# A chunked gated recurrence: two tree levels' matmuls per visit of the tensor engine, and two weight blocks split earlier and on another engine

## The chip, the cores and the metric

The kernel runs on one core of a Trainium2 chip. The time is device microseconds of one execution of the whole program. The kernel before takes 1827.11 us, the median of 3 runs (1826.62 to 1827.6).

## The reference, cut to what matters

The program is one step of a two-layer trunk on 640 tokens (128 context, 512 latent) of width 1024. Layer 0 mixes tokens by attention, layer 1 by a gated linear recurrence (HGRN2); each is followed by a dense feed-forward part. The change is inside layer 1's mixer. Cut to its core, the reference computes there, for each of 8 heads and for both directions:

```python
def chunk_gla(q, k, v, lf, s0):            # c = 16 tokens a chunk
    b = jnp.cumsum(lf, axis=2)             # lf = log(f), f the forget gate, k = 1 - f
    dec = exp(b[t] - b[s])  for s <= t
    a = sum(q[t] * k[s] * dec, over dk)    # all pairs inside a chunk
    o = a @ v + (q * exp(b)) @ s_start     # pairs inside, and the state before
    s = exp(b_last) * s + (k * exp(b_last - b)).T @ v
def hgrn_project(h, w_in, lb):
    q, vi, g, zf, zb = split(h @ w_in, 5)  # query, value, output gate, two forget gates
    f = lb + (1 - lb) * sigmoid(z)
def hgrn_mix(...):                         # forward scan plus the scan of the reversed tokens
```

Any chunk length gives the same result, and the kernel uses chunks of 128 tokens.

## The kernel before, in words

All of `hgrn` (line 1029) handles one head at a time: 128 channels on the partitions, 640 tokens in five tiles of 128 on the free axis. `project` (1040) makes a head's inputs, and `core` (1123) computes its recurrence. Both are generators. While `core(h)` of one head runs, `project(h + 1)` of the next is the filler: each `yield n` of `core` makes the loop at 1285 take `n` units of the filler. TensorE runs in exactly the order in which the program issues it (`pe["strict"]`), so these numbers are TensorE's order. The other engines' orders are chosen by a scheduler at build time; each engine then runs its queue strictly in that order.

**Weights.** Matmuls with weights keep close to float32 accuracy by splitting each raw block `wr` into a high part `wh` (`AC.activation`, ScalarE, ACT in the profile) and a low part `wl = wr - wh` (`split_raw`, 197), and using three products. The low part goes to GpSimd (POOL) in three pieces, or to VectorE (DVE) in one. A head has five blocks of 128x1024: two `ch` (query and forward gate), one `chb` (backward gate), two `cg` (value and output gate). There are 6 buffers each for `wh` and `wl`.

**The filler.** `project` makes six products `psf` of 24 matmuls (two halves of the tokens; query, forward gate, backward gate), each in 4 units, then five `psvg` (values and gates) of 24 matmuls, also 4 units each: 44 units. After a `psf`, ACT takes the sigmoid `sg`, and DVE makes `q`, or else the gate `F2`, the key `CD = 1 - F2` and the query times the gate, `Q2`. After a `psvg`, ACT copies `v` and takes the gate's sigmoid, and DVE multiplies (`gt`). `load_cg` (1053) for a head other than the first stands after the last `psf`. `psf` and `psvg` share 3 PSUM buffers.

**The recurrence.** `core` builds the 128x128 score matrix `A` of each token tile as a binary tree. First come the diagonal's products ("base": `q` with `kd`), then for levels li = 0 to 6 the pairs of neighbouring blocks of 2^li tokens: keys `C` times queries from `Q2`, 20 small matmuls of 32 columns (10 of 64 at level 6) into the PSUM tile `pa` (two buffers). Base and each level are one *visit* of TensorE, with 4 units of filler behind it: eight visits. After a level's products DVE folds its decays in: `Cn` (two instructions, two buffers), `CD`, and `Q2` in place, for which the level's products must have been read; and puts the level into `A` with `copy_predicated`. Levels 5 and 6 go into `A` by ACT, with copies of one part by POOL. POOL multiplies the decays of pairs (`T2`).

After level 6 come the transposes `ktp` in three groups (one PSUM buffer, read by ACT into `KT2`), then `pk` (the states) and five `po` (the output). POOL computes `rs`, and DVE writes the head's output `orow`.

**The last head** has no next projection: its filler is `part_units` (562), 22 units that turn `orow` (transposes `otp`, ACT's `Thi`, DVE's `Tlo`) and multiply with the output weights (`psr`, matmuls of 512 columns). The loop at 1303 takes 2 units a visit, 1 in some.

Names in the profile lose their numbers: `Q` is `Q2`, `F` is `F2`, `T` is `T2`, `KT` is `KT2`. Nearly all instructions of ACT, DVE and POOL carry line 51, and all matmuls line 96 (transposes 99), so a row is told by its tiles.

Of the kernel before, what the change touches and what calls it, by code (L numbers as in the profile page):

```python
# [21 lines left out]
P = 128  # L22
D = 1024
KT = D // P
NT = 5
# [34 lines left out]
def trunk_kernel(ctx: ExitStack, tc: tile.TileContext, I, O):  # L60
# [136 lines left out]
    def split_raw(r, lo_eng, ordered=False):  # L197
        n = r.shape[1]
        hi = wp.tile([P, 1024], F32R, name="wh", tag="wh", bufs=6)
        lo = wp.tile([P, 1024], F32R, name="wl", tag="wl", bufs=6)  # L200
        AC.activation(hi[:, :n], r, AF.Copy)
        parts = 3 if lo_eng is PO else 1
        for i in range(parts):
            cs = slice(n * i // parts, n * (i + 1) // parts)
            ins = lo_eng.tensor_tensor(lo[:, cs], r[:, cs], hi[:, cs], ALU.subtract)
            if ordered:
                tc.keep_in_program_order(ins)
        return hi[:, :n], lo[:, :n]
# [820 lines left out]
    def hgrn(regB, hT, o_tiles, xr):  # L1029
        with ExitStack() as sc:  # L1030
# [9 lines left out]
            def project(h):  # L1040
# [32 lines left out]
                if h == 0:  # L1073
                    load_cg()
# [43 lines left out]
                if h:  # L1118
                    load_cg()
# [3 lines left out]
            def core(h):  # L1123
# [4 lines left out]
                def pair_products(w, keys, queries):  # L1128
                    pa = psB.tile([P, 1024], F32, name="pa", tag="pa", bufs=2)
# [12 lines left out]
                def across(w):  # L1142
                    def queries(t, b):
                        c0 = t * P + w * (b ^ 1)
                        return Q2[:, 1 - b % 2, c0 : c0 + w]

                    return queries

                pa = pair_products(32, kd, lambda t, b: q[:, t * P + 32 * b : t * P + 32 * b + 32])
                AC.activation(Ad, pa, AF.Copy)  # L1150
                S = {}
                for d in range(2):
                    s0 = rp.tile([P, P], F32, name="s0", tag="S", bufs=8)
                    nc.sync.dma_start(out=s0, in_=st[d, h])
                    S[d, 1 if d == 0 else NT - 1] = s0
                yield 4
                T, n = F2, TOK
                C, Dk = CD[:, 0], CD[:, 1]
                for li in range(7):
# [3 lines left out]
                    qdims = ([2 * m, nb], [TOK + m, 2], [1, m])  # L1163
                    qview = view(Q2, 0, *qdims)
                    if li < 5:
                        bt = 32 // (2 * m)
                        pa = pair_products(32, C, lambda t, b: qview[:, (4 * t + b) * bt : (4 * t + b + 1) * bt])
                    else:
                        pa = pair_products(m, C, across(m))
                    if li < 6:  # L1170
                        Cn = rp.tile([P, TOK], F32, name="Cn", tag="Cn", bufs=2)
# [13 lines left out]
                        VE.tensor_tensor(  # L1185
                            qview, qview, view(T, n + 1, [2, nb], [-n - 1, 2], [0, m]), ALU.mult
                        )
                    else:
                        Cn = rp.tile([P, TOK], F32, name="Cn", tag="Cn", bufs=2)
# [6 lines left out]
                        VE.tensor_tensor(  # L1196
                            qview, qview, view(T, n + 1, [2, nb], [-n - 1, 2], [0, m]), ALU.mult
                        )
                    if li < 5:
                        VE.copy_predicated(Ad, masks[:, li, :].unsqueeze(1).to_broadcast([P, NT, 32]), pa)  # L1200
                    else:
                        for b in range(P // m):
                            rs_, own, other = slice(m * b, m * b + m), slice(0, m), slice(m, 2 * m)
                            if b % 2:
                                PO.tensor_copy(A[rs_, :, other], A[rs_, :, own])
                                AC.activation(A[rs_, :, own], pa[rs_], AF.Copy)
                            else:
                                AC.activation(A[rs_, :, other], pa[rs_], AF.Copy)
# [3 lines left out]
                    T, n, C = T2, nb, Cn  # L1212
                    yield 4
# [787 lines left out]
```

## Time and profile before

| | |
|---|---|
| median of 3 runs | 1827.11 us |
| profiled execution | 1824.8 us |
| its span | 1823.0 us |
| granted TensorE clock | 0.998 |
| busy share of the span: PE / DVE / ACT / POOL | 97% / 67% / 41% / 35% |
| recurrence, from the first head's base visit to the last one's | 958.1 to 1295.6 us |
| one head there | 48.2 us |

The last two rows are from the timeline of TensorE; the first head's base visit is its row that starts at 958.11. In a timeline row stand the start, the time from the first start to the last end of the instructions in it, the engine, the line, the operation, output and inputs, shape, the count, and in brackets how long the engine was idle before and what released it. A small float32 matmul counts twice (x40 for 20). A matmul's row lasts to its modelled end, while the next one starts before: how fast TensorE goes is read from starts. A windows row gives, for a stretch, its length, and each engine's busy time with the number of its instructions.

### The profile page before, as it was taken

To read this page: it belongs to the slowest core of one execution; us is meant where nothing else is said; L and a number is where in the kernel's file an instruction comes from. 1 tells how busy PE (TensorE), PEld (TensorE's weight loads), DVE (VectorE), ACT (ScalarE), POOL (GpSimd) and SP (SyncE) were. 2 spreads that over 40 slices of the span, in tenths; PEclk is the share of its full clock that TensorE was granted. 3 is DMA by queue.
4 is the path that set the end of the run, shared out by engine and by line. 5 is a ranking of instruction groups with operands and counts; after the bars stand their busy time and mean duration, and the time that the engine had idled before them with its cause. 6 is when DMAs were issued, how large, how long until landed. Compare 5 with 4: busy or idle time off the path is not lost.

```text
span 1823.0 us, 34717 instructions
## 1 busy us (share of the span) xinstructions
PE 1770.5 (97%) x13791; PEld 1626.0 (89%) x13791; DVE 1219.6 (67%) x2128; ACT 742.0 (41%) x1642; POOL 643.0 (35%) x750
## 2 busy tenths in 40 slices
PE   6999999999999999999999999999999999999997
PEld 5799999878898899899899999999879898998896
DVE  4888888756266755855667766666759656566666
ACT  3567666635132122122353333333345443433443
POOL 3344544325000000000056554444411557366562
PEclk9999999999999999999999999999999999999999
DMA  9511221454264534453442222211222324233331
GB/s 317 180 44 45 70 62 39 168 185 122 90 202 138 150 106 133 143 152 122 145 128 67 62 63 65 59 60 58 84 84 82 104 82 116 81 99 110 93 104 70
DMA packets 222857, 195.28 MB, mean 107 GB/s; under 512 B 10276, under 2 KB 176606, under 8 KB 222694
## 3 DMA queue, kind: packets, MB, share of 16 engines
q1 hardware_dynamic: 221888, 192.46, 34.2%
q8 instruction: 108, 1.77, 0.4%
q10 hardware_dynamic: 806, 0.60, 0.1%
q14 instruction: 55, 0.45, 0.1%
HBM read 185.64 MB, written 7.37 MB: 106 GB/s over the span
## 4 chain that ended last, share of the span: by engine, by line
PE 81%; DVE 9%; DMA 4%; issue 2%; ACT 2%; POOL 1%; SPq 0%; POOLq 0%; DVEq 0%; ACTq 0%
PE psgu L96 22%; PE psr L96 19%; PE psf L96 8%; PE psqkv L96 8%; PE psvg L96 5%; PE psu L96 4%; PE pso L96 2%; PE S L96 2%; PE psg L96 2%; PE pa L96 2%; PE po L96 1%; DMA wr<-w_ada 1%; DVE wl L51 1%; DMA ar<-w_ada 1%; DVE Q L51 1%
## 5 line engine op out<-in xcount | busy, mean ns | idle before, releaser
L51 ACT ACTIVATE wh<-wr 128x1024 fp32r<-128x1024 f32 (+2 forms) x224 | 217.1, 976 | 381.3 <-DMA wr<-w_ffn_in 110.6
L51 DVE TENSOR_TENSOR wl<-wr,wh 128x1024 fp32r<-128x1024 f32 (+2 forms) x148 | 178.9, 1213 | 185.7 <-ACT wh L51 184.5
L96 PE MATMUL psgu<-Thi,wh 128*128 128x320 f32 x880 | 272.7, 311 | 2.1 <-ACT wh L51 2.0
L96 PE MATMUL psgu<-Tlo,wh 128*128 128x320 f32 x880 | 271.8, 309 | 2.3 <-DVE Tlo L51 2.3
L96 PE MATMUL psgu<-Thi,wl 128*128 128x320 f32 x880 | 270.8, 309 | 0.7 <-DVE wl L51 0.7
L51 POOL TENSOR_TENSOR wl<-wr,wh 128x341 fp32r<-128x341 f32 (+2 forms) x228 | 212.8, 964 | 161.8 <-ACT wh L51 161.2
L96 PEld LDWEIGHTS psgu<-Thi,wh 128*128 128x128 f32 x880 | 165.1, 188 | 5.3 <-ACT wh L51 2.8
L51 POOL TENSOR_TENSOR nss<-nss 128x1 f32<-128x1 f32 x24 | 8.3, 345 | 455.7 <-ACT xr L51 438.8
L96 PEld LDWEIGHTS psgu<-Tlo,wh 128*128 128x128 f32 x880 | 165.1, 188 | 3.7 <-DVE Tlo L51 2.8
L96 PEld LDWEIGHTS psgu<-Thi,wl 128*128 128x128 f32 x880 | 164.7, 188 | 1.9 <-DVE wl L51 1.4
L96 PE MATMUL psr<-wh,Thi 128*128 128x512 f32 x380 | 152.6, 404 | 0.5 <-ACT Thi L51 0.5
L96 PE MATMUL psr<-wh,Tlo 128*128 128x512 f32 x380 | 148.6, 391 | 0.0
L96 PE MATMUL psr<-wl,Thi 128*128 128x512 f32 x380 | 148.3, 390 | 0.0
L96 PE MATMUL psr<-wh,gT 128*128 128x512 f32 (+1 forms) x448 | 140.5, 388 | 1.0 <-DVE gT L51 0.7
L96 PE MATMUL psf<-Thi,wh 128*128 128x320 f32 x384 | 123.1, 321 | 0.0
L51 DVE SCALAR_TENSOR_TENSOR acc<-wr,cT,acc 128x512 f32<-128x512 f32 x168 | 116.3, 746 | 6.4 <-DMA wr<-w_ada 6.4
L96 PE MATMUL psf<-Thi,wl 128*128 128x320 f32 x384 | 118.5, 308 | 0.0
L96 PE MATMUL psf<-Tlo,wh 128*128 128x320 f32 x384 | 118.4, 308 | 0.0
L96 PE MATMUL psqkv<-wh,Thi 128*128 128x384 f32 x320 | 109.1, 356 | 1.2 <-ACT Thi L51 1.2
L96 PE MATMUL psqkv<-wh,Tlo 128*128 128x384 f32 x320 | 104.3, 339 | 0.5 <-DVE Tlo L51 0.5
L96 PE MATMUL psqkv<-wl,Thi 128*128 128x384 f32 x320 | 103.7, 339 | 0.0
L51 DVE TENSOR_TENSOR rtmp<-psr,gate 128x512 f32<-128x512 f32 (+1 forms) x101 | 66.1, 679 | 55.8 <-PE psr L96 42.8
(288 smaller groups left out, 4668.3 us busy)
## 6 DMA issues: line engine op xcount, KB each, us to landing
wr<-w_ffn_in SPq DMA_DIRECT2D x176, 256.0 KB
wr<-w_ada SPq DMA_DIRECT2D x72, 512.0 KB
wr<-w_ffn_out SPq DMA_DIRECT2D x40, 512.0 KB
wr<-w_in_rec SPq DMA_DIRECT2D x64, 256.0 KB
wr<-w_qkv_attn SPq DMA_DIRECT2D x64, 192.0 KB
ar<-w_ada SPq DMA_DIRECT2D x24, 512.0 KB
gate<-gdram SPq DMA_DIRECT2D x28, 256.0 KB
wr<-w_o_attn SPq DMA_DIRECT2D x8, 512.0 KB
```

What stands on the lines that cost most here:

```text
L51: ins = op(*a, **k)
L96: in_order(nc.tensor.matmul(*a, **k))
```

## The change

It edits three things.

1. `core` makes four visits instead of eight, each with the products of two levels: base and 0, 1 and 2, 3 and 4, 5 and 6, with 9, 9, 9 and 5 units behind them. Both levels of a visit share one `pa` tile, one in each half. For a level's products to be done later than its decays are folded into `Q2`, ACT first copies its queries into a new buffer `QV` (640 columns, one buffer, three copies a head); the keys are kept too, as `C` before the step. So after a visit two steps run on DVE, with an ACT copy between the two multiplications of `Q2`.
2. For heads after the first, the two `cg` blocks are loaded and split at the third and fourth `psf`, before they stood behind the sixth.
3. Their low parts go to DVE in two halves of 512 columns, before to POOL in three pieces.

The loops that take units by the number of the visit (1285, 1303) are not edited. With fewer visits the four pieces of the output weights `w_o[0]` that are loaded in the next-to-last head at visits 2, 4, 6, 8 come later in it, and the last head still takes 2 units behind each of the first three visits.

The diff, cut:

```diff
@@ split_raw
-        parts = 3 if lo_eng is PO else 1
+        parts = parts or (3 if lo_eng is PO else 1)
@@ project
-                def load_cg():
-                    for c in range(2):
-                        cg.append(load_split(wr[:, 4 * c : 4 * c + 4, 1:3, h, :], [4, 2, P], lo_eng))
+                def load_cg(c):
+                    r = load_raw(wr[:, 4 * c : 4 * c + 4, 1:3, h, :], [4, 2, P])
+                    cg.append(split_raw(r, VE, parts=2 if h else 1))
...
+                        if h and (half, which) in ((0, 2), (1, 0)):
+                            load_cg(half)
...
-                if h:
-                    load_cg()
@@ core
+                S = {}
...
+                kept, QV = None, None
+                for first, units in ((-1, 9), (1, 9), (3, 9), (5, 5)):
+                    pa = psB.tile([P, 1024], F32, name="pa", tag="pa", bufs=2)
+                    if first < 0:
+                        own = pair_products(
+                            pa, 32, kd, lambda t, b: q[:, t * P + 32 * b : t * P + 32 * b + 32]
+                        )
+                        AC.activation(Ad, own, AF.Copy)
+                    else:
+                        put_level(first, level_products(first, pa, kept, QV))
+                    crossed = level_products(first + 1, pa[:, 512:], C)
+                    C, T, n = step(first + 1, C, T, n)
+                    put_level(first + 1, crossed)
+                    li = first + 2
+                    if li < 7:
+                        QV = rp.tile([P, TOK], F32, name="QV", tag="QV", bufs=1)
+                        AC.activation(
+                            QV.rearrange("p (b s i) -> p b s i", s=2, i=1 << li), crossing(li), AF.Copy
+                        )
+                        kept = C
+                        C, T, n = step(li, C, T, n)
+                    yield units
```

`step` holds the four DVE instructions of a level and POOL's `T2`, unchanged (two `Cn`, `CD`, `Q2`; at level 6 one `Cn` and `Q2`); `put_level` is what puts a level into `A`; `crossing` is the view of `Q2` with one level's queries. `level_products` is `pair_products` for one level, with `QV` where it is given.

**Three places in the orders.** First TensorE at the start of the last head, where the filler is short (`pa` are the products, `otp` and `psr` the filler). Before:

```order
L96 MATMUL pa<-q,kd 32x32 x20
L99 MATMUL otp<-ident,orow 128x128 x11
L96 MATMUL pa<-Q_14839,CD 32x32 x20
L96 MATMUL psr<-wh,Thi 128x512
L96 MATMUL psr<-wl,Thi 128x512
```

and now:

```order
L96 MATMUL pa<-q,kd 32x32 x20
L96 MATMUL pa<-Q_14876,CD 32x32 x20
L99 MATMUL otp<-ident,orow 128x128 x11
L96 MATMUL pa<-QV,Cn 32x32 x20
L96 MATMUL pa<-Q_14876,Cn 32x32 x20
L96 MATMUL psr<-wh,Thi 128x512
```

Levels 1 and 2, which need the steps of levels 0 and 1, now stand ahead of the first `psr`; before, level 0 stood there and level 1 came after two units of `psr`.

Second DVE in the third head, from level 5's `Cn` on (`Q_11469` or `Q_11506` is the running head's `Q2`; `F_12144` or `F_12181` the next head's gate; `Cn` 128x640 is level 6's). Before:

```order
L51 TENSOR_TENSOR Cn<-Cn,T_12464 128x5x2x32
L51 COPY Cn<-CD 128x5x64
L51 TENSOR_SCALAR F_12144<-sg,omlb,lb 128x320
L51 TENSOR_TENSOR CD<-Cn,T_12464 128x5x64
L51 TENSOR_SCALAR CD<-F_12144 128x160x2
L51 TENSOR_TENSOR Q_12143<-q,F_12144 128x320
L51 TENSOR_TENSOR Q_11469<-Q_11469,T_12464 128x10x2x32
L51 TENSOR_TENSOR Cn<-Cn,T_12528 128x640
L51 TENSOR_SCALAR F_12144<-sg,omlb,lb 128x320
```

and now:

```order
L51 TENSOR_TENSOR Cn<-Cn,T_12463 128x5x2x32
L51 COPY Cn<-CD 128x5x64
L51 TENSOR_TENSOR Q_11506<-Q_11506,T_12463 128x10x2x32
L51 TENSOR_TENSOR CD<-Cn,T_12463 128x5x64
L51 TENSOR_SCALAR F_12181<-sg,omlb,lb 128x320
L51 TENSOR_SCALAR CD<-F_12181 128x160x2
L51 TENSOR_TENSOR Q_12180<-q,F_12181 128x320
L51 TENSOR_TENSOR wl<-wr,wh 128x512 x2
L51 TENSOR_SCALAR F_12181<-sg,omlb,lb 128x320
L51 TENSOR_TENSOR Cn<-Cn,T_12473 128x640
```

Level 5's `Q2` now stands ahead of the next head's instructions, and level 6's `Cn` behind them, with a `cg` block's low part and the second gate `F` between.

Third POOL at the same place (`A` 32x5x32 and 64x5x64 are the copies of levels 5 and 6, `T` from `F` is the next head's first decay product). Before:

```order
L51 COPY A<-A 32x5x32 x2
L51 TENSOR_TENSOR wl<-wr,wh 128x341 x2
L51 TENSOR_TENSOR wl<-wr,wh 128x342
L51 COPY A<-A 64x5x64
L51 TENSOR_TENSOR T_12904<-F_12144 128x640
```

and now:

```order
L51 COPY A<-A 32x5x32 x2
L51 TENSOR_TENSOR wl<-wr,wh 128x341 x2
L51 TENSOR_TENSOR wl<-wr,wh 128x342
L51 TENSOR_TENSOR T_12841<-F_12181 128x640
L51 COPY A<-A 64x5x64
```

Level 6's copy now stands behind `T`, which waits for the next head's last `F`; the `wl` ahead of them is now the next but one head's `chb`, before it was a `cg` block. ACT's part of level 6 in turn follows that copy, and stands ahead of `KT2`.

More of the change, by code (lines that the diff above doesn't have):

```diff
@@ L195, in load_split, with split_raw @@
         return split_raw(load_raw(src, dims, slots), lo_eng, ordered)
-    def split_raw(r, lo_eng, ordered=False):
+    def split_raw(r, lo_eng, ordered=False, parts=None):
         n = r.shape[1]
@@ L1073, in project @@
                 if h == 0:
-                    load_cg()
+                    for c in range(2):
+                        load_cg(c)
                 ch = [load_split(wr[:, 4 * c : 4 * c + 4, 0:4:3, h, :], [4, 2, P], lo_eng) for c in range(2)]
@@ L1116, in project @@
                 PO.tensor_tensor(kd, CD[:, 0], CD[:, 1], ALU.add)
-                if h:
-                    load_cg()
                 for t in range(0 if h else 2, NT):
@@ L1126, in core, with pair_products @@
                 Ad = A[:, :, 0:32]
-                def pair_products(w, keys, queries):
-                    pa = psB.tile([P, 1024], F32, name="pa", tag="pa", bufs=2)
+                def pair_products(pa, w, keys, queries):
                     for t in range(NT):
@@ L1140, in pair_products, with crossing, level_products, step @@
                     return pa[:, : NT * w].rearrange("p (t s) -> p t s", t=NT)
-                def across(w):
-                    def queries(t, b):
[L1144 to L1159, printed above, removed]
+                def crossing(li):
+                    m = 1 << li
+                    return view(Q2, 0, [2 * m, TOK // (2 * m)], [TOK + m, 2], [1, m])
+                def level_products(li, pa, keys, packed=None):
+                    m = 1 << li
+                    bt = 32 // (2 * m)
+                    def queries(t, b):
+                        if li < 5:
+                            if packed is not None:
+                                return packed[:, t * P + 32 * b : t * P + 32 * b + 32]
+                            return crossing(li)[:, (4 * t + b) * bt : (4 * t + b + 1) * bt]
+                        c0 = t * P + m * (b ^ 1)
+                        src = Q2[:, 1 - b % 2] if packed is None else packed
+                        return src[:, c0 : c0 + m]
+                    return pair_products(pa, max(m, 32) if li >= 5 else 32, keys, queries)
+                def step(li, C, T, n):
                     m = 1 << li
@@ L1162, in core @@
                     q4 = nb // 2
[L1163 to L1169, printed above, removed]
+                    qview = crossing(li)
+                    Cn = rp.tile([P, TOK], F32, name="Cn", tag="Cn", bufs=2)
                     if li < 6:
-                        Cn = rp.tile([P, TOK], F32, name="Cn", tag="Cn", bufs=2)
                         mid, outer = ([4 * m, q4], [m, 2], [1, m]), ([4 * m, q4], [3 * m, 2], [1, m])
@@ L1184, in core @@
                         )
-                        VE.tensor_tensor(
-                            qview, qview, view(T, n + 1, [2, nb], [-n - 1, 2], [0, m]), ALU.mult
-                        )
                     else:
-                        Cn = rp.tile([P, TOK], F32, name="Cn", tag="Cn", bufs=2)
                         VE.tensor_tensor(
@@ L1195, in core @@
                         )
[L1196 to L1208, printed above, removed]
+                    VE.tensor_tensor(qview, qview, view(T, n + 1, [2, nb], [-n - 1, 2], [0, m]), ALU.mult)
                     T2 = rp.tile([P, 2, nb], F32, name="T2", tag=f"T{li}", bufs=1)
@@ L1211, in core, with put_level @@
                     PO.tensor_tensor(T2, tv[:, :, :, 0], tv[:, :, :, 1], ALU.mult)
-                    T, n, C = T2, nb, Cn
-                    yield 4
+                    return Cn, T2, nb
+                def put_level(li, pa):
+                    m = 1 << li
+                    if li < 5:
+                        VE.copy_predicated(Ad, masks[:, li, :].unsqueeze(1).to_broadcast([P, NT, 32]), pa)
+                        return
+                    for b in range(P // m):
+                        rs_, own, other = slice(m * b, m * b + m), slice(0, m), slice(m, 2 * m)
+                        if b % 2:
+                            PO.tensor_copy(A[rs_, :, other], A[rs_, :, own])
+                            AC.activation(A[rs_, :, own], pa[rs_], AF.Copy)
+                        else:
+                            AC.activation(A[rs_, :, other], pa[rs_], AF.Copy)
@@ new lines, in core @@
+                S = {}
+                for d in range(2):
+                    s0 = rp.tile([P, P], F32, name="s0", tag="S", bufs=8)
+                    nc.sync.dma_start(out=s0, in_=st[d, h])
+                    S[d, 1 if d == 0 else NT - 1] = s0
+                T, n = F2, TOK
+                C, Dk = CD[:, 0], CD[:, 1]
+                kept, QV = None, None
[6 more added lines that the diff above has]
+                        AC.activation(Ad, own, AF.Copy)
+                    else:
+                        put_level(first, level_products(first, pa, kept, QV))
[11 more added lines that the diff above has]
+                    yield units
```

## The prediction

> **What bounds the kernel now.** I read the busy times by stretch first, for the third head from its base visit to the next one's (this head is the clock for all below: t = 0 is 1054.55). Columns: length, busy time of PE, PEld, DVE, ACT and POOL.
>
> ```profile
> 1054.55:1102.75 48.20, 47.39 (x617) 45.20 (x617) 32.95 (x61) 17.12 (x46) 25.04 (x29) 1.00 0.22 62
> ```
>
> TensorE (PE) is busy for 47.39 of 48.20 us and DVE for 32.95. So time is won only where TensorE does less or waits less. Second, TensorE's own waits from 955 to 1340 us:
>
> ```profile
> PE pa L96 <- DVE Q L51: 5.7, 7, 0.8
> PE otp L99 <- DVE orow L51: 1.6, 1, 1.6
> PE po L96 <- ACT jk L51: 1.0, 2, 0.5
> PE ktp L99 <- ACT KT L51: 0.6, 1, 0.6
> ```
>
> One wait of 0.8 us in each of seven heads, and 3.2 us in the last head. Third, TensorE's timeline around a visit:
>
> ```profile
> 1066.71 0.31 PE L96 MATMUL psf<-Thi,wh 128*128 128x320 f32 x1
> 1066.85 0.31 PE L96 MATMUL psf<-Tlo,wh 128*128 128x320 f32 x1
> 1067.00 0.31 PE L96 MATMUL psf<-Thi,wl 128*128 128x320 f32 x1
> 1067.24 0.56 PE L96 MATMUL pa<-Q,Cn 128*32 128x32 f32 x40
> 1067.73 0.42 PE L96 MATMUL psf<-Thi,wh 128*128 128x320 f32 x1
> 1067.99 0.31 PE L96 MATMUL psf<-Tlo,wh 128*128 128x320 f32 x1
> ```
>
> Matmuls of the filler start 0.147 us apart. From 1067.00 to 1067.99 two such steps would take 0.29; it is 0.99, so a visit costs 0.70 us. Its 20 products take 0.56 less the last one's own length of about 0.19 (0.31 of a psf row is twice its spacing in the same way), so 0.37. The other 0.33 is the change of kind: there, back, and the slower first matmul.
>
> **The visits that go.** Joining two visits saves about 0.32 us; the second level's products still cost 0.37. Four a head: 1.28 us, in seven heads 9.0 us. In the order, the joined products do stand together, so that the change does what it says is no question.
>
> One page would make this more. The Trainium skill, TensorE: Matmul & The Clock Gate, "The mechanism", puts about 4 ns between small products that lie on different parts of the array, which for 40 passes is an estimate of 0.16 us. By it the joined level would cost 0.16 instead of 0.37 and the sum would gain 28 x 0.21 = 5.9 us more. The row disagrees: its 40 passes take 0.37, so 9 ns each, and I keep that.
>
> **The wait at level 6.** The next rows hold it, and the first transposes behind it:
>
> ```profile
> 1084.17 0.80 PE L96 MATMUL pa<-Q,Cn 128*64 128x64 f32 x20 [0.81 <-DVE Q L51]
> ...
> 1087.84 0.27 PE L99 MATMUL ktp<-ident,Cn 128*128 128x128 f32 x1
> ...
> 1089.73 0.33 PE L99 MATMUL ktp<-ident,Cn 128*128 128x128 f32 x1
> ```
>
> It waits for level 5's `Q2`, which on DVE comes late because POOL works at the same time. DVE without and with POOL:
>
> ```profile
> 1072.43 0.82 DVE L51 TENSOR_TENSOR Q<-Q,T 128x640 f32<-128x640 f32 x1
> 1073.17 0.33 DVE L51 COPY_PREDICATED A<-masks,pa 128x160 f32<-128x160 uint8 x1
> 1073.40 0.48 DVE L51 TENSOR_TENSOR Cn<-Cn,T 128x320 f32<-128x320 f32 x1
> 1073.80 0.32 DVE L51 COPY Cn<-CD 128x320 f32<-128x320 f32 x1
> 1074.16 0.49 DVE L51 TENSOR_TENSOR CD<-Cn,T 128x320 f32<-128x320 f32 x1
> ...
> 1077.63 0.99 DVE L51 TENSOR_TENSOR Cn<-Cn,T 128x320 f32<-128x320 f32 x1
> 1078.54 1.07 DVE L51 COPY Cn<-CD 128x320 f32<-128x320 f32 x1
> 1079.54 0.98 DVE L51 TENSOR_SCALAR F<-sg,omlb,lb 128x320 f32<-128x320 f32 x1
> 1080.44 1.21 DVE L51 TENSOR_TENSOR CD<-Cn,T 128x320 f32<-128x320 f32 x1
> 1081.57 0.57 DVE L51 TENSOR_SCALAR CD<-F 128x320 f32<-128x320 f32 x1
> 1081.98 0.68 DVE L51 TENSOR_TENSOR Q<-q,F 128x320 f32<-128x320 f32 x1
> 1082.58 1.54 DVE L51 TENSOR_TENSOR Q<-Q,T 128x640 f32<-128x640 f32 x1
> ```
>
> A step of four takes 1.8 us alone (0.40 + 0.24 + 0.40 + 0.73 by starts) and about 4.5 beside POOL. POOL and ACT behind it:
>
> ```profile
> 1075.00 6.29 POOL L51 TENSOR_TENSOR wl<-wr,wh 128x341 fp32r<-128x341 f32 x6 [15.38 <-ACT wh L51]
> 1081.36 0.95 POOL L51 COPY A<-A 32x160 f32<-32x160 f32 x2
> 1082.40 3.96 POOL L51 TENSOR_TENSOR wl<-wr,wh 128x341 fp32r<-128x341 f32 x3
> 1086.42 0.45 POOL L51 COPY A<-A 64x320 f32<-64x320 f32 x1
> 1086.95 1.27 POOL L51 TENSOR_TENSOR T<-F 128x640 f32<-128x640 f32 x1
> ```
>
> ```profile
> 1086.90 0.43 ACT L51 ACTIVATE A<-pa 64x320 f32<-64x320 f32 x1 [1.45 <-POOL A L51]
> ...
> 1088.48 1.20 ACT L51 ACTIVATE KT<-ktp 64x512 f32<-64x512 f32 x2
> ```
>
> Now the walk with the change (times from t = 0 are estimates from these rows). Visits cost 0.70 + 0.37 = 1.07 and a `psf` unit 6 x 0.147 = 0.88, so levels 3 and 4 come at 2 x 1.07 + 18 x 0.88 = 18.0. DVE starts at 18.6, when level 3 is read. Until Q2 of step 5 it has two puts (0.23), two `Cn` pairs, one `CD`, two `Q2`; alone 3.6 us, all of it beside POOL 8.4. POOL has three `wl` pieces there (3.96 at most, from the release of a `ch` buffer just before 18.2), so about the first half is slowed: I take 6, so 24.6; the ends are 22.2 and 27.0. ACT's copy `QV` lies between the two `Q2`; a 640-column copy is not in the trace; from 0.43 at 320 and 0.60 at 512 columns I take 0.7, and it runs beside DVE's put, `Cn` and copy and costs nothing (uncovered, 0.7 a visit). The next visit comes at 18.0 + 1.07 + 6 x 0.88 + 3 x 0.7 = 26.5 (a `psvg` unit is 0.7: from 1087.84 to 1089.73 lie two of them and four transposes). Level 6 there needs `Q2` at 26.9. So the 0.81 goes in each of seven heads, 5.7 us, and even at 27.0 the loss is 0.1. The copies before the second and third visit have more room, since there POOL rests (idle for 15.38 us ahead of 1075.00).
>
> **What is late next.** `KT2`. Before the transposes, TensorE's program is shorter by 1.28 + 0.81, so the first group comes at 33.3 - 2.1 = 31.2 and the second at 33.1, 1.9 later. The second needs the one PSUM buffer back, so ACT's `KT2`. In the new order that stands behind ACT's part of level 6, which waits for POOL's copy of `A`, which stands behind `T`, which waits for DVE's last `F`. On DVE ahead of that `F` stand now `CD`, `F`, the next head's `CD` and `Q2`, and the two halves of `wl` moved from POOL. A half's row:
>
> ```profile
> L51 DVE TENSOR_TENSOR wl<-wr,wh x148: 678/1226/2319, 21.1 to 1789.5; 128x1024 fp32r<-128x1024 f32 x115, 128x512 fp32r<-128x512 f32 x28, 128x768 fp32r<-128x768 f32 x5
> ```
>
> Its shortest, 0.68, is a half alone, and 1.2 is my estimate for one beside POOL. From 24.6: `CD` 0.5, `F` 0.9, `CD` 0.4, `Q2` 0.8, `wl` 1.5, `F` 0.4 gives 29.1 (POOL's next three pieces lie over the first of these). Then `T` 1.27, copy 0.45, ACT's part 0.43, two short ACT rows 0.5, `KT2` 1.20: 3.9, so 33.0 to 33.5 against 33.1. I take a wait of 0.4 us, in six heads 2.4 us. From both sides: with everything alone there is none, and with all beside POOL `F` ends at 33.3 and the wait is 4.1.
>
> The seventh head differs: there POOL has two `wl` of the output weights in that place, and ACT's part of level 6 stands behind both, `T` and `kd` (as wide as `T`). Three pieces are 3.96 at most, 3.3 as I take it; from 24.5, 2 x 3.3 + 1.3 + 1.3 + 0.45 + 0.4 + 1.2 gives 35.7, so a wait of 2.6 (0 to 4.5).
>
> **The last head.** Its filler behind a visit is short, and each visit now needs two steps. DVE at its start before:
>
> ```profile
> 1298.57 1.38 DVE L51 SCALAR_TENSOR_TENSOR orow<-po,rs,gt 128x128 f32<-128x128 f32 x5
> 1299.87 1.27 DVE L51 SCALAR_TENSOR_TENSOR Tlo<-otp,vcol,Thi 128x512 fp32r<-128x512 f32 x2
> 1301.05 1.37 DVE L51 TENSOR_TENSOR Q<-Q,F 128x640 f32<-128x640 f32 x1
> ```
>
> Now five `orow`, `Q2` of step 0, a put, three `Tlo`, `Q2` of step 1 stand in a row before level 2: 1.3 + 1.3 + 0.25 + 1.85 + 0.75 = 5.4. The first `orow` began 3.0 after the base visit at 1295.6, behind a `Tlo` (0.6) that now comes later, so from 2.4 to 7.8; in it TensorE has only transposes and level 1, an estimated 2.7 us of work. That is 5.1 us idle where it was 1.6. The second visit should find its queries ready (12 `psr` in between); the third, with 9, waits some 0.9. The three small waits at the end (`po`, `ktp`, 1.6 us) go, since the 22 units now last to the end. So 6.0 idle against 3.2, less 1.3 for four joined visits: 1.5 us lost (0 to 5).
>
> **Sum.** -9.0 - 5.7 + 2.4 + 2.6 + 1.5 = -8.2 us, on the profiled execution's 1824.8 (1816.6). The median of the runs shown is 2.3 higher, so I forecast 1827.1 - 8.2 = 1818.9 us. About 0.2%, 3.7 us, is what can be told from no change.
>
> **Rivals.**
> *POOL holds DVE back longer than the wait removed* (slower). If POOL's pieces stretch every DVE instruction between level 3 and the last `F`, the wait at the second transposes is 4.1 us a head against the 2.1 won, 7 x 2.0 + 1.5 = +15.5, 1842.6. It decides from where that `F` ends after about 31. For it: the rows beside POOL, two to four times as long, and 1.4 us more DVE work at just this place. Against it: POOL has two of its five blocks less per head, and before it worked from 1075.00 through 1086 almost without a stop. The Trainium skill, SBUF — State Buffer, "Who interferes with whom", says that a DVE instruction with two SBUF inputs and a GpSimd instruction that reads SBUF exclude each other for the whole instruction; by that the halves of `wl` on DVE also hold up POOL's pieces ahead of `T`, which would favour this rival. The rows of DVE beside POOL agree with it.
> *Given back* (same). The wait is 1.5 us in each of six heads and the last head loses 4: -14.7 + 9 + 2.6 + 4 = +0.9, 1828.0.
> *No new wait* (faster still). The slack suffices everywhere, the last head comes out even: -14.7, 1812.4.
>
> **How the numbers follow.** Forecast 0.60, no new wait 0.14, given back 0.17, DVE held back 0.09. Faster: 0.60 + 0.14 = 0.74. The range leaves out the slow rival and the far ends: 1812 to 1828.
>
> **What would show it.** Right: base visits 46.5 us apart (48.2 less 1.7); `pa` x80 where x40 stood; no `pa` that waits for `Q` but in the last head; a wait of `ktp` for `KT` under 1 us, 2 to 3 in the seventh head. Wrong: heads that stay at 48, with `ktp` or `psvg` waiting for DVE or ACT; a visit in the first seven heads that waits for `QV`; more than 5 us lost after the last base visit.

## The result, and the profile after

The changed kernel takes 1852.19 us (median of 4 runs, 1848.17 to 1855.36) against 1826.86 us for the kernel before (median of 4, 1825.18 to 1827.6). The ratio is 1.0141, 95% interval 1.0129 to 1.0154: it is slower by 25 us, where 8 us less was forecast.

The profiled execution took 1851.25 us, with a span of 1849.3 against 1823.0. The 26.3 us between the spans lie as follows, by the starts of the base visits (`pa<-q,kd`) in both traces:

| stretch | before | after | difference |
|---|---|---|---|
| start to the first base visit | 958.1 | 959.8 | 1.7 |
| heads 1 to 6, base visit to base visit | 48.2 each | 50.55 each | 14.0 in all |
| seventh head | 48.2 | 52.5 | 4.3 |
| last base visit to the feed-forward's first product | 81.7 | 87.2 | 5.5 |
| from there to the end | 445.7 | 446.5 | 0.8 |

So nearly all of it is lost inside the heads. The busy times of the third head after (length, PE, PEld, DVE, ACT, POOL, granted clock, DMA):

```profile
1060.93:1111.47 50.54, 46.93 (x617) 45.28 (x616) 35.71 (x65) 19.36 (x49) 19.64 (x23) 1.00 0.21 59
```

TensorE works 46.93 us where it worked 47.39, as a kernel with cheaper visits should, but it now stands idle for 3.6 us of each head. Its own waits from 955 to 1380 us (us in total, times, longest) say for what:

```profile
PE pa L96 <- ACT A L51: 20.0, 16, 1.3
PE pa L96 <- DVE A L51: 9.7, 16, 1.3
PE pa L96 <- ACT QV L51: 2.6, 1, 2.6
PE ktp L99 <- ACT KT L51: 1.8, 1, 1.8
PE psr L96 <- DVE orow L51: 0.8, 1, 0.8
```

The row that the change was to remove, `pa <- DVE Q`, is gone. In its place stand 32 waits of `pa` for `A`, four in each of eight heads, 29.7 us together. No such row stood in the kernel before. TensorE's timeline shows where they are; first the base visit, then levels 1 and 2 with the filler's products around them, then level 4 and level 6:

```profile
1060.93 0.56 PE L96 MATMUL pa<-q,kd 128*32 128x32 f32 x40
1062.68 0.63 PE L96 MATMUL pa<-Q,CD 128*32 128x32 f32 x40 [1.19 <-ACT A L51]
...
1071.13 0.31 PE L96 MATMUL psf<-Thi,wl 128*128 128x320 f32 x1
1071.37 0.56 PE L96 MATMUL pa<-QV,Cn 128*32 128x32 f32 x40
1072.61 0.56 PE L96 MATMUL pa<-Q,Cn 128*32 128x32 f32 x40 [0.68 <-DVE A L51]
1073.10 0.41 PE L96 MATMUL psf<-Thi,wh 128*128 128x320 f32 x1
...
1082.21 0.56 PE L96 MATMUL pa<-Q,Cn 128*32 128x32 f32 x40 [0.43 <-DVE A L51]
...
1092.18 0.80 PE L96 MATMUL pa<-Q,Cn 128*64 128x64 f32 x20 [1.32 <-ACT A L51]
```

The two levels of a visit are not joined. The twenty products of the first level run (forty passes, x40 in the row), then TensorE waits, then the second twenty run. What it waits for is the reading of the *first* level out of `pa`. On DVE that is the put of level 1, on ACT the base visit's copy, behind a weight split, and level 5's four copies:

```profile
1072.23 0.32 DVE L51 COPY_PREDICATED A<-masks,pa 128x160 f32<-128x160 uint8 x1
```

```profile
1061.38 1.06 ACT L51 ACTIVATE wh<-wr 128x1024 fp32r<-128x1024 f32 x1
1062.35 0.28 ACT L51 ACTIVATE A<-pa 128x160 f32<-128x160 f32 x1
...
1090.90 1.23 ACT L51 ACTIVATE A<-pa 32x160 f32<-32x160 f32 x4 [1.38 <-PE pa L96]
```

Each of the second levels starts a moment after the end of such a row (1072.23 + 0.32 = 1072.55, then 1072.61). The two levels write different halves of the tile, 512 columns apart, but the code makes one tile of them, writes the first half, reads it, and only then writes the second half; the wait is put on the tile. A wait costs more than its row says: from the last product before it to the first behind it lie 0.87 us at level 2 (1071.37 + 0.37 to 1072.61) where the row says 0.68. The row counts from the last pass's modelled end, and a pass is shown 0.20 long, so each wait costs 0.2 more than its row. Four waits (1.19, 0.68, 0.43 and 1.32) and four times 0.2 are 4.4 us a head, and 46.1 (48.2 less 1.28 less 0.81, the forecast's head without waits) plus 4.4 is 50.5: the head as measured.

### The profile page after: what moved, and what is told of

The parts are those of the page before. It is cut to its first block, busy times and chain, and to the rows that moved or that the text cites. A ratio compares the mean times of both kernels' runs of the same rounds, so it can differ in the third digit from the quotient of the medians.

```text
span 1849.3 us, 34731 instructions
## 1 busy us (share of the span) xinstructions
PE 1769.1 (96%) x13791; PEld 1629.3 (88%) x13791; DVE 1241.0 (67%) x2156; ACT 759.3 (41%) x1666; POOL 607.8 (33%) x708
## 4 chain that ended last, share of the span: by engine, by line
PE 80%; DVE 7%; DMA 5%; ACT 3%; POOL 2%; issue 2%; SPq 0%; POOLq 0%; DVEq 0%; ACTq 0%
PE psgu L96 22%; PE psr L96 19%; PE psf L96 9%; PE psqkv L96 8%; PE psvg L96 6%; PE psu L96 4%; PE pso L96 2%; PE S L96 2%; PE psg L96 2%; PE pa L96 1%; PE po L96 1%; DVE wl L51 1%; POOL wl L51 1%; ACT wh L51 1%; PE ptp L99 1%
## 5 line engine op out<-in xcount | busy, mean ns | idle before, releaser
L51 DVE TENSOR_TENSOR wl<-wr,wh 128x1024 fp32r<-128x1024 f32 (+2 forms) x176 | 197.3, 1131 | 206.0 <-ACT wh L51 204.2
L51 POOL TENSOR_TENSOR wl<-wr,wh 128x341 fp32r<-128x341 f32 (+1 forms) x186 | 172.2, 955 | 158.1 <-ACT wh L51 148.3
```

The source lines that it names most:

```text
L51: ins = op(*a, **k)
```

## The experiments

All kernels with their times, ratios to the kernel before with 95% intervals, and the base-visit distances of their profiles (heads 2 to 6 where nothing else is said, the seventh head, and from the last base visit to the feed-forward's first product):

| kernel | us | ratio | head | seventh | last |
|---|---|---|---|---|---|
| before | 1826.86 | 1 | 48.2 | 48.2 | 81.7 |
| after | 1852.19 | 1.0129 to 1.0154 | 50.55 | 52.5 | 87.2 |
| both products first | 1832.36 | 1.0019 to 1.0045 | 48.3 (third 49.8) | 49.0 | 86.0 |
| tiles of one bank | 1829.33 | 1.0001 to 1.0020 | 47.4 | 50.6 | 86.5 |
| weights alone | 1821.96 | 0.9971 to 0.9991 | 47.4 | 48.1 | 81.7 |
| visits alone | 1865.94 | 1.0196 to 1.0227 | 52.5 | 52.5 | 87.4 |
| level 6 put late | 1829.86 | 0.9998 to 1.0022 | 47.4 | 50.4 | 85.8 |
| counts of the last heads too | 1829.37 | 0.9999 to 1.0022 | 47.4 | 49.2 | 85.2 |
| before with tiles of one bank | 1825.93 | 0.9989 to 1.0008 | 48.0 | 48.0 | 80.9 |
| level 6's copy on ACT | 1825.46 | 0.9980 to 1.0000 | 47.1 | 50.6 | 85.4 |
| joined in six heads only | 1821.50 | 0.9958 to 0.9982 | 47.1 | 48.1 | 82.5 |
| six heads, gate copied by ACT | 1815.60 | 0.9925 to 0.9957 | 46.25 | 48.2 | 82.5 |
| six heads, low parts on GpSimd | 1839.03 | 1.0048 to 1.0081 | 50.8 (sixth 49.4) | 48.0 | 80.9 |
| gate copied by ACT, no head joined | 1824.24 | 0.9967 to 0.9986 | 47.4 | 48.2 | 82.7 |

**Both products ahead of the reading.** The shared tile stays; only the first level's reading is written behind the second level's products.

```diff
+                    else:
+                        own = level_products(first, pa, kept, QV)
+                    crossed = level_products(first + 1, pa[:, 512:], C)
+                    if first < 0:
                         AC.activation(Ad, own, AF.Copy)
                     else:
-                        put_level(first, level_products(first, pa, kept, QV))
-                    crossed = level_products(first + 1, pa[:, 512:], C)
+                        put_level(first, own)
```

> The changed kernel, but in each visit the products of both levels are written ahead of the reading of the first level into A; the tile stays shared. Theory (the loss is TensorE's wait, inside each visit, for the first level to be read out of the tile that the second level writes too; 3.6 us a head and some 0.4 of restarts): those waits vanish, base visits come 46.3 to 47.0 us apart instead of 50.5, time 1819 to 1826. Rival 1 (the wait only hides another: the queries of the second level, or the transposes behind KT2, are late as well): heads stay at 48.5 or more, with a pa that waits for Q or QV or a ktp that waits for KT by 1 us or more, time 1835 to 1850. Rival 2 (the loss is DVE's extra work on the weights): time within 3 us of the changed kernel's 1852.

Measured: 1832.36 us, 20 us less than the changed kernel, and no `pa` waits for `A` any more. The weights on DVE are unchanged, so rival 2 is out: the wait at the tile was the loss. But heads come 48.3 apart, not 46.3 to 47.0, and rival 1 has its row:

```profile
PE ktp L99 <- ACT KT L51: 11.6, 6, 2.0
```

A new wait of 1.9 us a head stands at the second transposes, the place that the prediction named. The time lies between the range of the theory and that of rival 1, and each holds a part: the waits for `A` were the loss, and behind them `KT` is late as well.

**A tile of one bank for each level.** The order of the changed kernel is kept.

```diff
-                    pa = psB.tile([P, 1024], F32, name="pa", tag="pa", bufs=2)
+                    pa = psB.tile([P, 512], F32, name="pa", tag="pa", bufs=4)
+                    pb = psB.tile([P, 512], F32, name="pb", tag="pa", bufs=4)
...
-                    crossed = level_products(first + 1, pa[:, 512:], C)
+                    crossed = level_products(first + 1, pb, C)
```

`pk`, `po` and the transposes at the start, which had the same two-bank tiles, are split into two tiles as well.

> The changed kernel in its own order, but the two levels of a visit have a PSUM tile of one bank each (four such tiles in place of two of two banks; the state products and the output rows are split in the same way). Theory (the wait is for the shared tile): the waits inside visits vanish, base visits 46.3 to 47.0 apart, time within 3 us of the kernel with both products first, 1819 to 1827. Rival 1 (the wait would also come with tiles of their own, since what is waited for is the order of the work and not the tile): waits of 0.4 to 1.3 us inside visits stay, time 1845 to 1855. Rival 2 (the splitting of the other tiles costs by itself): waits inside visits gone, but new ones on the state products or the output rows, 1828 or more.

Measured: 1829.33 us, 23 us less than the changed kernel. So it is the tile and not the order as such. TensorE's timeline of levels 1 and 2 of a head, and its waits:

```profile
1111.68 0.53 PE L96 MATMUL pa<-QV,Cn 128*32 128x32 f32 x38
...
1112.06 0.54 PE L96 MATMUL pb<-Q,Cn 128*32 128x32 f32 x38
1112.53 0.41 PE L96 MATMUL psf<-Thi,wh 128*128 128x320 f32 x1
```

```profile
PE ktp L99 <- ACT KT L51: 7.3, 6, 1.3
```

The forty products run through in about 0.73 us from the first start to the last (1112.06 + 0.54 less the last pass's 0.20). By the starts of the filler around it, the visit with both levels costs 1.05 us, where two single visits cost 0.70 each; so a join saves 0.35, close to the forecast's 0.32. What gives it back is the wait of 1.2 to 1.3 us at `ktp`: 46.1 + 1.2 = 47.3 against 47.4 measured, where 46.3 to 47.0 were expected. ACT shows why:

```profile
1135.21 0.43 ACT L51 ACTIVATE A<-pb 64x320 f32<-64x320 f32 x1 [3.38 <-POOL A L51]
...
1135.98 1.19 ACT L51 ACTIVATE KT<-ktp 64x512 f32<-64x512 f32 x2
```

ACT stands still 3.38 us for GpSimd's copy within `A`, with `KT` queued behind it. (With both products first, GpSimd made `kd`, 1.66 us, between `T` and that copy, and the wait was 1.9; whether that is the whole difference was not followed.) The time, 1829.33, is in rival 2's range; a control answers that rival:

**The kernel before with tiles of one bank.** The same split of `pa` (one level at a time), `pk`, `po` and those transposes in the kernel before, nothing else.

> The kernel before with the tiles of one bank alone: eight visits as before, weights as before. Theory (without a second level in the tile there is nothing to gain, and the splitting costs nothing): within 2 us of the kernel before. Rival (the shared two-bank tiles cost something in the kernel before as well, or splitting them does): 3 us or more either way.

Measured: ratio 0.9989 to 1.0008. The split alone changes no time that can be told; heads are 0.2 us shorter in its profile.

**The two parts of the change by themselves.** First the weights in the kernel before, then the visits with the weights as before.

```diff
-                def load_cg():
-                    for c in range(2):
-                        cg.append(load_split(wr[:, 4 * c : 4 * c + 4, 1:3, h, :], [4, 2, P], lo_eng))
+                def load_cg(c):
+                    r = load_raw(wr[:, 4 * c : 4 * c + 4, 1:3, h, :], [4, 2, P])
+                    cg.append(split_raw(r, VE, parts=2 if h else 1))
```

> The kernel before with the value and gate weights alone changed: loaded amid the projections, low parts in two halves on DVE. Theory (this part takes away the wait at level 6, 0.81 in seven heads, and costs little on DVE): 1821 to 1825 against 1826.9. Rival (the DVE halves make other DVE work late): 1828 to 1834, with ktp or psvg waiting for DVE or ACT.

Measured: 1821.96 us, ratio 0.9971 to 0.9991. Heads are 47.4, 0.8 us shorter, and level 6's wait is gone in the first six heads; in the seventh 0.7 us of it stay. So six sevenths of the term of -5.7 us are to be had without the visits.

> The changed kernel with the value and gate weights as before (loaded after the projections, low parts in thirds on GpSimd). Theory (the loss is all in the joined visits): 1849 to 1858, and the waits inside visits as in the changed kernel, 3.6 us a head. Rival (the weights part is the loss): 1820 to 1830.

Measured: 1865.94 us, worse than the changed kernel by 14 us, so slower than the 1849 to 1858 expected. The waits for `A` are the same (20.0 and 9.9 us), as the theory said, and this row is larger than in the changed kernel:

```profile
PE ktp L99 <- ACT KT L51: 12.8, 7, 1.9
```

So the loss is the joined visits', and the weights part had hidden some of it: without it the wait at `ktp` comes on top, 1.8 us in seven heads.

**Level 6's put behind KT2.** With tiles of one bank, `put_level(6, ...)` is written behind the loop that makes `KT2`.

> The changed kernel with tiles of one bank, and with the put of level 6 into A written behind the transposes and copies into KT2 instead of ahead of them. In the run with tiles of one bank the second transposes waited 1.3 us a head for ACT's KT, which stood behind ACT's part of level 6, which waited 3.4 us for GpSimd's copy of A. Theory (that order on ACT is what gives the joined visits' gain back): no ktp waits for KT in heads 1 to 6, base visits 46.1 apart instead of 47.4, and 1819 to 1823 against 1829. Rival (the KT copies are late for another reason, such as Cn of step 6 on DVE, or the wait moves on to the output rows that need A): base visits 46.8 or more apart, 1825 or more.

Measured: 1829.86 us, heads 47.4 as without it. The edit didn't bring about what it was for: the program has the put later, but ACT's queue, whose order the scheduler chooses, still has its part of level 6 ahead of `KT`:

```profile
1136.75 0.43 ACT L51 ACTIVATE A<-pb 64x320 f32<-64x320 f32 x1 [3.38 <-POOL A L51]
...
1137.53 1.19 ACT L51 ACTIVATE KT<-ktp 64x512 f32<-64x512 f32 x2
```

It decides nothing about the theory.

**The counts of the last two heads.** The kernel just shown, with the first pair of output weights behind the seventh head's second visit, and 4, 3, 3, 2 units of filler at the last head's visits.

```diff
-                    if h == H - 2 and i in (2, 4, 6, 8):
-                        w_o[0] += w_chunks(wo, i - 2, 2, 0, PO)
+                    if h == H - 2 and i in (1, 4, 6, 8):
+                        w_o[0] += w_chunks(wo, 0 if i == 1 else i - 2, 2, 0, PO)
...
-                take(fill, 1 if i == 3 or i > 8 else 2)
+                take(fill, (4, 3, 3, 2, 1, 1, 1, 2, 1, 1, 1, 1, 1)[i])
```

> As the kernel with the put of level 6 behind KT2, and besides the places in the last two heads that count visits are fitted to four visits instead of eight: the first pair of output weights comes behind the second visit of the seventh head, and the last head takes 4, 3, 3, 2 units of filler at its visits. Theory (the seventh head's 3 us and the last head's 5 us are lost because these counts were made for eight visits): seventh head 46 to 47.5 instead of 50.6, last base visit to the feed-forward's first product 81 to 83 instead of 86.5, time 1812 to 1817. Rival (the last head is bound by the chain of steps on DVE, and the units only run out at another place): last head 85 or more, 1816 to 1821.

Measured: 1829.37 us, the same time. The seventh head still waits 2.92 us at its first transposes for DVE's `Cn`, as with tiles of one bank alone, and the last head is 85.2 long. Yet the seventh head is 1.4 us shorter than with tiles of one bank alone. The wait and the five microseconds around its end, with tiles of one bank:

```profile
1279.23 0.33 PE L99 MATMUL ktp<-ident,Cn 128*128 128x128 f32 x1 [2.92 <-DVE Cn L51]
```

```profile
1280.00:1285.00 5.00, 5.00 (x32) 5.00 (x31) 3.08 (x7) 2.87 (x7) 2.84 (x5) 0.66 0.00 0
```

and with the new counts:

```profile
1281.33 0.33 PE L99 MATMUL ktp<-ident,Cn 128*128 128x128 f32 x1 [2.92 <-DVE Cn L51]
```

```profile
1280.00:1285.00 5.00, 3.67 (x31) 3.60 (x32) 5.00 (x7) 2.53 (x5) 4.61 (x6) 1.00 0.02 8
```

The wait is the same; the granted clock behind it (the column after POOL) is 0.66 in the one and 1.00 in the other. So the shorter head is not the counts' doing by any wait that the rows show, and the theory fell: the expected 1812 to 1817 did not come, nor the rival's 1816 to 1821, though its last head of 85 or more did. What the seventh head waits for is DVE's `Cn` of level 6. With tiles of one bank it starts late and runs long, behind six instructions for the next head, while GpSimd splits weights beside them:

```profile
1277.03 2.15 DVE L51 TENSOR_TENSOR Cn<-Cn,T 128x640 f32<-128x640 f32 x1
```

```profile
1268.47 6.58 POOL L51 TENSOR_TENSOR wl<-wr,wh 128x341 fp32r<-128x341 f32 x6
```

In the fourth head of the same profile, where GpSimd has half as many pieces there, the same `Cn` took 0.82.

**Level 6's copy on ACT.** With tiles of one bank, ACT copies within `A` itself and no longer waits for GpSimd.

```diff
-                            PO.tensor_copy(A[rs_, :, other], A[rs_, :, own])
+                            if li == 6:
+                                AC.activation(A[rs_, :, other], A[rs_, :, own], AF.Copy)
+                            else:
+                                PO.tensor_copy(A[rs_, :, other], A[rs_, :, own])
```

> The changed kernel with tiles of one bank, and with level 6's copy within A (64x320) on ACT instead of GpSimd, so that ACT no longer stands still for GpSimd ahead of the KT copies (writing the put later had left ACT's order as it was). ACT gets about 0.4 us more work a head. Theory (that wait of ACT, 3.4 us a head, is what holds the second transposes): no ktp waits for KT in heads 1 to 6, base visits 46.0 to 46.3 apart instead of 47.4, the seventh head and the last one as they were (50 and 86), time 1819 to 1823. Rival (KT is late for another reason): base visits 47 or more apart, 1826 to 1830.

Measured: 1825.46 us, and no `ktp` waits for `KT`. But heads are 47.1, not the theory's 46.0 to 46.3. That is the rival's 47 or more, though not for the rival's reason, and the time lies between the two: the wait has moved. Three microseconds behind the start of the second transposes, TensorE waits for a `psvg` buffer that DVE's gate product holds, and on DVE that product stands behind level 6's `Q2` and the next head's first two `Cn` instructions:

```profile
1134.74 0.38 PE L96 MATMUL psvg<-wh,Thi 128*128 128x256 f32 x1 [0.66 <-DVE gt L51]
```

```profile
1130.59 2.19 DVE L51 TENSOR_TENSOR Q<-Q,T 128x640 f32<-128x640 f32 x1
1132.70 1.29 DVE L51 TENSOR_TENSOR Cn<-CD,F 128x320 f32<-128x320 f32 x1
1133.90 0.58 DVE L51 COPY Cn<-CD 128x320 f32<-128x320 f32 x1
1134.41 0.28 DVE L51 TENSOR_TENSOR gt<-psvg,gt 128x128 f32<-128x128 f32 x1
```

**Joined in six heads only.** The last two heads get eight single visits again, each with a tile of one bank.

```diff
-                for first, units in ((-1, 9), (1, 9), (3, 9), (5, 5)):
+                for first, units in ((-1, 9), (1, 9), (3, 9), (5, 5)) if h < H - 2 else ():
...
+                for li in range(-1, 7) if h >= H - 2 else ():
...
+                        crossed = level_products(li, pa, C)
+                        C, T, n = step(li, C, T, n)
+                        put_level(li, crossed)
+                    yield 4
```

> As the kernel with level 6's copy on ACT, but the last two heads keep eight single visits of four units as the kernel before has them; only heads 1 to 6 have joined visits. Theory (joining pays 1.3 us a head where the filler is long enough and costs in the last two heads, where TensorE stands idle for 2 to 3 us at a time and its granted clock then falls to 0.5 to 0.7): heads 1 to 6 46.0 to 46.3, seventh head 47.5 to 48.2, last head to the feed-forward 81 to 82, time 1811 to 1816, ahead of both kernels and of the weights alone (1822). Rival (the gain in heads 1 to 6 shows up as a later wait at the change to the single visits): 1817 to 1822.

Measured: 1821.50 us. The last two heads came out nearly as the theory says (48.1, and 82.5 against 85.4 where 81 to 82 were expected). Heads 1 to 6 kept the wait at `psvg` and their 47.1, so the total is in the rival's range.

**The gate copied by ACT.** One wait more taken away: ACT copies the gate half out of PSUM, and DVE multiplies from SBUF.

```diff
-                    VE.tensor_tensor(gt[:, t], ps[:, P:], gt[:, t], ALU.mult)
+                    g0 = rp.tile([P, P], F32, name="g0", tag="g0", bufs=3)
+                    AC.activation(g0, ps[:, P:], AF.Copy)
+                    VE.tensor_tensor(gt[:, t], g0, gt[:, t], ALU.mult)
```

> The kernel with joined visits in heads 1 to 6, and the gate half of the value and gate tile copied out of PSUM by ACT (128x128, five a head), so that DVE multiplies from SBUF and no longer holds that tile. With level 6's copy on ACT the wait of 1.3 us at ktp had gone, and a wait of 0.7 at psvg for DVE's gt had come 2 us later in its place. Theory (the joined visits set DVE's work closer behind TensorE than before, and whatever TensorE needs from DVE's queue there is late): no psvg waits for gt, base visits 46.2 to 46.4 apart in heads 1 to 6 instead of 47.1, 1815 to 1818. Rival (the wait moves on once more, to pk, po or the next base visit): base visits 46.8 or more, 1819 to 1823.

Measured: 1815.60 us, ratio 0.9925 to 0.9957, faster than both kernels. A head of its profile has no idle time of TensorE left:

```profile
1049.39:1095.63 46.24, 46.24 (x618) 45.00 (x617) 35.12 (x65) 20.71 (x55) 20.92 (x22) 1.00 0.22 64
```

46.24 is 0.1 from the 46.1 that the forecast's two gains give.

**The low parts back on GpSimd.** The kernel with six joined heads (without the gate's copy), the value and gate weights split amid the projections as in the change, but the low parts in thirds on GpSimd.

```diff
-                    cg.append(split_raw(r, VE, parts=2 if h else 1))
+                    cg.append(split_raw(r, lo_eng))
```

> The kernel with joined visits in heads 1 to 6, with the low parts of the value and gate weights back on GpSimd in thirds, but at the new place amid the projections. It tells the place of that work from its engine. Theory (the engine counts: GpSimd's thirds slow DVE's instructions beside them two- to threefold, which costs more than 1.3 us twice on DVE): base visits 48 or more apart in heads 1 to 6, 1827 or more. Rival (the place alone counts, and DVE without these halves is earlier with gt): base visits 46.5 to 47.1, 1817 to 1822.

Measured: 1839.03 us, 17 us behind. The engine counts. In the six joined heads `ktp` waits for DVE:

```profile
PE ktp L99 <- DVE Cn L51: 17.8, 6, 3.0
```

and GpSimd works almost without a stop ahead of it, beside the end of DVE's step 5 and the next head's instructions, where the kernel with halves on DVE had three pieces:

```profile
1082.76 6.57 POOL L51 TENSOR_TENSOR wl<-wr,wh 128x341 fp32r<-128x341 f32 x6
```

It is the same wait as in the seventh head above. It is 3.0 us in each of the six heads, yet the first and the sixth are 49.4 long and the four between them 50.8. The stretches behind it in the second head and in the sixth (the column after POOL is the granted clock):

```profile
1042.70:1046.20 3.50, 3.50 (x17) 3.50 (x18) 3.50 (x6) 1.19 (x2) 3.15 (x5) 0.51 0.00 0
1245.90:1249.40 3.50, 3.48 (x29) 3.40 (x30) 3.50 (x6) 2.02 (x4) 3.19 (x5) 1.00 0.00 0
```

In the third to fifth heads it is 0.56 to 0.66, in the first 1.00. So of the 3.7 us by which the heads between are longer than 47.1, the wait is 2.3 and the clock behind it 1.4.

**No head joined.** The 1815.60 us kernel with single visits in all heads (`h < 0` in place of `h < H - 2`).

> As the kernel with the gate copied by ACT, but with single visits in all eight heads: tiles of one bank, weights amid the projections, level 6's copy and the gate's copy on ACT stay. It tells what the joining itself pays. Theory (four joined visits a head save 4 x 0.33 = 1.3 us in six heads, and nothing else of the difference is theirs): base visits 47.4 to 47.6 apart against 46.25, and 1821 to 1825, 7 to 8 us behind the kernel with joined visits in six heads (1815.6). Rival (the copies on ACT make the gain, and would without joining): base visits 46.5 or less, 1815 to 1818.

Measured: 1824.24 us, heads 47.4 against 46.25. The ratios are 0.9977 and 0.9941, 6.6 us apart by 1827; six heads of 1.18 us are 7.1. So the joining itself pays 1.2 us a head, and the copies on ACT gain nothing without it (heads are 47.4 with the weights alone, too).

## Why the prediction was wrong, point by point

**The visits that go (forecast -9.0): the step that failed.** "Joining two visits saves about 0.32 us; the second level's products still cost 0.37" took it for granted that the second level runs straight behind the first. The saving is about right (0.35 in a visit with tiles of one bank, and 1.18 a head between the last two kernels where 1.28 was forecast), and so are 9 ns a pass. The order showed that the two levels stand together, not that the second may start. In the changed kernel the second level writes into the tile that the first has yet to be read from. That costs 4.4 us a head, of which the prediction had nothing and no rival had anything. Both ways of taking it away, by order and by tile, gave back 20 and 23 of the 25 us. The program could have shown it: the first level is read between the two sets of products, and both go to one `pa`.

**The wait at level 6 (forecast -5.7): right.** No product of the first seven heads waits for `Q`, with tiles of one bank neither, where TensorE isn't held up ahead of level 6. There level 5's `Q2` in the fourth head ended 25.3 after the base visit, where the walk had 24.6. The weights alone do it in six of the seven heads, each 0.8 shorter, and are 1.6 to 5.3 us faster by their ratio.

**The second transposes (forecast +0.4 in each of six heads): right in kind, too small.** In the changed kernel the wait isn't there, because TensorE comes some 4 us later. With tiles of one bank it is 1.2, by the chain that was named, here on DVE and GpSimd ahead of ACT's rows above:

```profile
1131.94 0.44 DVE L51 TENSOR_SCALAR F<-sg,omlb,lb 128x320 f32<-128x320 f32 x1
```

```profile
1132.46 2.05 POOL L51 TENSOR_TENSOR T<-F 128x640 f32<-128x640 f32 x1 [2.62 <-DVE F L51]
1134.58 0.60 POOL L51 COPY A<-A 64x320 f32<-64x320 f32 x1
```

The base visit was at 1102.65, so `F` ended at 29.7 after it, not 29.1; `T` took 2.05 beside DVE's work, not 1.27, the copy 0.60, not 0.45. The 7.3 us of the six waits in place of 2.4 would have made the forecast without the tile's wait -3.3. The gate behind `psvg` on DVE, which the last experiments found next, was not in the walk at all.

**The seventh head (forecast +2.6).** Its own wait in the changed kernel is 1.8, with the four tile waits before it. That one is at the second transposes for `KT`, as forecast. With tiles of one bank it is 2.9 at the first transposes, for DVE's `Cn`, not 2.6 at the second for `KT`. So the size agrees by luck: the walk gave GpSimd's two blocks of output weights their time on GpSimd, but not what they do to DVE, which is the first rival's mechanism in one head.

**The last head (forecast +1.5, to 5 at most): 5.5.** Its waits are 7.8 us (1.2 and 1.3 on ACT's `A`, 1.3 and 0.6 on DVE's, 2.6 for `QV`, 0.8 behind) against 3.2 before. Most of the rest is the clock. Windows of five microseconds (the column behind POOL is the granted clock), and products of `psr` behind the idle time:

```profile
1316.00:1321.00 5.00, 2.13 (x66) 1.71 (x55) 3.26 (x8) 3.01 (x6) 4.83 (x6) 1.00 0.60 208
1321.00:1326.00 5.00, 2.74 (x83) 2.31 (x84) 4.97 (x13) 0.89 (x2) 0.67 (x1) 0.59 0.36 105
1326.00:1331.00 5.00, 4.83 (x57) 3.64 (x55) 3.06 (x7) 1.94 (x3) 0.00 (x0) 0.73 0.01 3
```

```profile
1327.65 0.63 PE L96 MATMUL psr<-wh,Tlo 128*128 128x512 f32 x1
1328.08 0.63 PE L96 MATMUL psr<-wh,Thi 128*128 128x512 f32 x1
...
1329.72 0.39 PE L96 MATMUL psr<-wl,Thi 128*128 128x512 f32 x1
1329.94 0.40 PE L96 MATMUL psr<-wh,Tlo 128*128 128x512 f32 x1
```

They start 0.43 apart and a little later 0.22. Some six at the wide spacing are an estimated 1.3 us. With the waits' 4.6 more, four times 0.2 as above and 1.3 less for the joins that makes 5.4. Nor is it the tile alone: with tiles of one bank this head still loses 4.9 (86.5 against 81.7). There the waits are 7.0, near the 6.0 of the forecast, and the clock is 0.60 and 0.71 for ten microseconds behind them. The forecast had no term for the clock.

**The rivals.** None held. The nearest mechanism was the first, GpSimd holding DVE back: with the low parts on GpSimd it is there, 3.0 us a head at `ktp`, and with tiles of one bank in the seventh head, but in the changed kernel it is not what costs the time. "Given back" is what the change would have come to with tiles of its own (1.0001 to 1.0020).

## What to carry to other kernels

When two stages are joined into one visit, look at what stands between them in the program: if the first one's result is read there out of a tile that the second also writes, the second may wait for that reading, as it did here, though the addresses don't meet. Taking a wait away moves TensorE ahead of every later one, and each is seen only when the one before is gone (here the tile, then `KT`, then `gt`); so a forecast has to walk on to the end of the head, with the durations that instructions have beside the other engines. Price a long idle time of TensorE above its length: here 1.4 to 1.5 us more where the clock fell behind it.

## What the runs showed of the hardware

TensorE's granted clock falls after idle time, though not each time. In the last head of the changed kernel TensorE was idle over half of five microseconds (2.13 busy), and the clock then was 0.59 and 0.73 for ten. With the low parts on GpSimd, the same wait of 3.0 us left it at 1.00 in two heads and was followed by 0.51 to 0.66 in four, each 1.4 us longer. With both products first, the wait of 1.9 to 2.0 us at `ktp` left the clock at 1.00 in the other joined heads with that wait, and in the third it fell to 0.61 behind it, for 1.5 us of the head's length (49.8 against 48.3). The stretches with the wait and behind it, in the second head and in the third:

```profile
1039.00:1042.50 3.50, 1.58 (x15) 1.45 (x14) 3.50 (x6) 1.66 (x4) 3.20 (x5) 1.00 0.02 6
1042.50:1046.00 3.50, 3.50 (x33) 3.42 (x32) 1.45 (x5) 1.58 (x6) 0.58 (x3) 1.00 0.00 0
...
1088.00:1091.50 3.50, 2.17 (x16) 2.17 (x17) 2.90 (x6) 2.10 (x4) 3.11 (x6) 0.90 0.00 0
1091.50:1095.00 3.50, 3.50 (x22) 3.50 (x21) 1.33 (x4) 1.18 (x4) 0.02 (x1) 0.61 0.00 0
```

The Trainium skill, TensorE: Matmul & The Clock Gate, "What's actually happening", says that the clock is halved after an idle window of about 3.4 us, and that the windows run freely and don't start with the kernel. The 0.43 against 0.22 us agrees with the half, and the same wait with and without a slow stretch behind it fits windows that run freely. The 3.4 us do not agree: the third head's wait of 1.9 us was enough here, and so was idle time in pieces.

The low part of one block cost 1.28 us as two halves on DVE, so two blocks 2.6 us a head. On GpSimd it made DVE late enough that a head grew by 2.3 us at the full clock (49.4 against 47.1), and by 3.7 where the clock fell.
